# The quarters' normalisations read the broadcast root from its PSUM bank instead of a copy in SBUF

## The chip, the cores and the metric

The kernel runs on one core of one Trainium2 chip. The metric is device time in microseconds (us). Five things work side by side on a core: TensorE (PE, matrix products, with its weight loads as a row of their own, PEld), VectorE (DVE), ScalarE (ACT), GpSimd (POOL) and the DMA queues, which SyncE (SP) issues. SBUF is the working memory; PSUM is the memory that matrix products are written to, in banks of 512 columns of float32.

## The reference

One inference step of a streaming encoder with two layers, in float32, on 1024 frames of a new stream and 64 frames of a running one, with 1024 channels. Layer 0 is a state space mixer followed by a SwiGLU feed forward net, layer 1 is attention over a band of chunks followed by another one. Around every sub-layer stand two normalisations (this is the part that the change touches):

```python
def rmsnorm(x, w):
    xf = x.astype(jnp.float32)
    y = xf * lax.rsqrt(jnp.mean(xf * xf, axis=-1, keepdims=True) + EPS)
    return (y * w.astype(jnp.float32)).astype(x.dtype)

def swiglu(u, w_in, w_out):
    g, up = jnp.split(u @ w_in, 2, axis=-1)
    return (jax.nn.silu(g) * up) @ w_out

# per layer: m is the mixer or the attention of rmsnorm(x, nw[0])
x = x + rmsnorm(m, nw[1])
x = x + rmsnorm(swiglu(rmsnorm(x, nw[2]), ffn_w_in, ffn_w_out), nw[3])
```

## The kernel before

Activations are kept transposed: channels on the 128 partitions, in eight tiles of 128 channels, and frames along the columns. All 1088 frames (1024 and 64) are columns of one product, cut into three slices of 384, 384 and 320 columns or, in the feed forward part, into four quarters `QS` of 256, 256, 288 and 288 columns. Every product of float32 numbers is made of three (`passes`, L487): weights and activations are each split into a high part and a rest, by a cast on ACT and a subtraction on DVE (the weights' at L366 and L367, the activations' at L1214 and L1215, L1708 and L1709, L1802 and L1803).

A normalisation of a quarter goes through these steps. ACT squares each of the eight channel tiles (L517, L521) and POOL, in some places DVE, adds the squares up (`add_sq`, L522). PE sums over the partitions by products with a column of ones into a small PSUM tile `nst` (L529). Ten short DVE operations make the reciprocal root of it (`rstd`, L536 to L547). DVE spreads the root on a diagonal (`diag`, L558), and PE multiplies the diagonal with a constant matrix, so that each partition holds the root of every column: `nbp`, a PSUM bank (`bcast`, L566). ACT copies it to SBUF (L574), into a tile `rb` of which there is one only (`bufs=1`). Then DVE multiplies each of the eight channel tiles by the norm's weight (a column, one number for each partition) and by `rb` in one operation. `rb_steps` (L577) puts these steps together.

This is done in three places:

- `chain` (L1251), at the start of each feed forward part, for each of four quarters twice: the post norm of the mixer with x added (L1273 multiplies, L1274 adds, on DVE for odd tiles and on POOL for even ones), then the pre norm of the feed forward net (L1285). The second half of x is fetched by a DMA (L1270) once the first half has been added.
- `EndU` (L1780), at the end of layer 0, for each quarter: the post norm (L1845) with x added (L1846), then the squares of the sum, its split for layer 1 (L1802, L1803), and the root for layer 1's first norm, which goes into SBUF tiles `rba` that live on (the form of `bcast` with a list, L572). The quarters come in the order 0, 2, 1, 3.
- `end7` (L1749), at the end of layer 1, for quarters 0, 2 and 3 (L1760 multiplies, L1761 adds). Quarter 1 ends the kernel in another way (L1659 to L1680).

PE's order of instructions is the order in which the program is written out. `Stream` interleaves side tasks with PE's main work by estimated times: a task yields (cost, delay, condition). The constants `CHW`, `ER_W`, `EP_W`, `EQ_W`, `ER7` are such delays, so that PE does a broadcast only when its root is likely to be there. The order on the other engines is made by a scheduler when the program is built; `tc.high_priority(k)` moves work forward in it by k. `CHP` is 300 or 1500 for the chains, `ENP` is 0, 1500, 0, 1500 for the quarters 0 to 3 at the end of layer 0, `OPP` 0 or 1200 for the sums and splits that make the operands of the feed forward products (`op_build`), and `W.pri` 0 or 3000 for the weights' splits. The roots themselves have 3000 (`HIP`).

PSUM has eight banks. Two are `mm` (`pmm`), two are `ax` (`pax`: `nst`, `nbp` and small things), and in the feed forward part four belong to `px`. There `mm` is used by the products of `run_pair` (two of their four banks, L1484) and by layer 1's first units (L2229), but not by the projections, by `plain_pairs` or by the second products in `wino`, which use `px`.

Of the kernel before, what the change touches and what calls it, by code (L numbers as in the profile page):

```python
# [17 lines left out]
D = 1024  # L18
# [34 lines left out]
EP_W, ER_W, EQ_W = (3.0, 3.0, 3.0), (5.5, 7.0, 5.5, 4.5), (18.0, 2.5, 14.0, 22.0)  # L53
EP7, ER7 = (3.0, 0.0, 3.0, 2.5), (5.0, 4.0, 5.0, 4.5)
# [356 lines left out]
def hybrid_kernel(  # L411
# [65 lines left out]
    def ax(name):  # L477
        return pax.tile([P, 512], F32, tag="ax", name=name)
# [45 lines left out]
    def rstd(ssum, inv, r, nb, more=None, pad=False):  # L524

        sp, ts = ax("nst"), [ssum] if more is None else [ssum, more]
        for i in range(nb):
            for j, t in enumerate(ts):
                PE.matmul(  # L529
                    sp[:, i:i + 1], t[:, i * P:(i + 1) * P], ones[:, 0:1], start=(j == 0), stop=(j == len(ts) - 1)  # L530
                )
        with tc.high_priority(2 * HIP if pad else HIP):
            v = nsb.tile([P, 12], F32, tag="nv", bufs=2, name="nv")
            a, h, y = v[:, 0:nb], v[:, 4:4 + nb], v[:, 8:8 + nb]
            steps = [
                lambda: V.tensor_scalar(a, sp[:, :nb], inv, EPS, op0=ALU.mult, op1=ALU.add),  # L536
                lambda: V.tensor_scalar(
                    y.bitcast(I32), a.bitcast(I32), -0.5, float(0x5F3759DF), op0=ALU.mult, op1=ALU.add
                ),
                lambda: V.tensor_tensor(h, y, y, op=ALU.mult),  # L540
                lambda: V.tensor_tensor(h, h, a, op=ALU.mult),
                lambda: V.scalar_tensor_tensor(h, h, -10.0 / 3.0, h, op0=ALU.add, op1=ALU.mult),
                lambda: V.scalar_tensor_tensor(y, h, 5.0, y, op0=ALU.add, op1=ALU.mult),
                lambda: V.tensor_tensor(h, y, y, op=ALU.mult),
                lambda: V.scalar_tensor_tensor(a, h, 9.0 / 64.0, a, op0=ALU.mult, op1=ALU.mult),
                lambda: V.scalar_tensor_tensor(h, a, -10.0 / 3.0, a, op0=ALU.add, op1=ALU.mult),
                lambda: V.scalar_tensor_tensor(r, h, 5.0, y, op0=ALU.add, op1=ALU.mult),  # L547
            ]
            for k, f in enumerate(steps):
                i = f()  # L550
                if pad and k < 9:
                    with tc.issue_after(i.ins):
                        for c in (3, 7):
                            V.memset(v[:, c:c + 1], 0.0)
# [7 lines left out]

    def bcast(dg, a, n, rb=None):

        bp = ax("nbp")
        PE.matmul(bp[:, :n], frac, dg.rearrange("p a b -> p (a b)")[:, a:a + n], start=True, stop=True)  # L566
        DG.put()
        if rb is None:
            rb = nsb.tile([P, 384], F32, tag="rb", bufs=1, name="rb")
        elif isinstance(rb, list):  # L570
            for d, c0, c1 in rb:
                A.copy(d, bp[:, c0:c1])  # L572
            return None
        A.copy(rb[:, :n], bp[:, :n])  # L574
        return rb[:, :n]

    def rb_steps(ssum, n, out, wait=None, rb=None, more=None):  # L577

        nb = (n + P - 1) // P
        nr = nsb.tile([P, 4], F32, tag="nr", bufs=2, name="nr")  # L580
        rstd(ssum, 1.0 / D, nr[:, :nb], nb, more, rb is None or more is not None or isinstance(rb, list))
        yield 0.2, 0, DG.free
        with tc.high_priority(HIP):
            dg = diag(nr[:, :nb], nb)
        yield 0.1, wait or RB_WAIT
        with tc.high_priority(HIP):
            out.append(bcast(dg, 0, n, rb))
        yield 0.5, 0
# [117 lines left out]
    with ExitStack() as es:  # L706
# [406 lines left out]
        for s in range(NSL):  # L1113
            us, n = u[s], SL[s][1]
# [27 lines left out]
        for grp in order:  # L1142
# [6 lines left out]
            for i, s in seq:  # L1149
                kd_, jj_ = grp[i]  # L1150
                q = 3 * jj_ + s
# [99 lines left out]
    def chain(layer, q, y, ss, cw, xsrc, xout, cpre, done):  # L1251

        o, n = QS[q]

        rings = (RX, R) if q < 2 else (R,)

        def some():
            return any(r.free() for r in rings)

        w_post, w_rb, w_pre = CHW[layer][q // 2]  # L1260
        yield 0, w_post, some
        t, r = take(*rings)
        xr = v4(t, n)
        nc.sync.dma_start(xr, xsrc[:, 0:4, o:o + n])
        out = []
        yield from rb_steps(ss, n, out, w_rb)
        s2 = ssum_start(n)
        for m in range(KD):
            if m == 4:
                nc.sync.dma_start(xr, xsrc[:, 4:8, o:o + n])  # L1270
            ym = y[m // 4][:, m % 4, :]
            with tc.high_priority(CHP[layer][q // 2]):
                V.scalar_tensor_tensor(ym, ym, col(cw + m), out[0], op0=ALU.mult, op1=ALU.mult)  # L1273
                (V if m % 2 else G).tensor_tensor(ym, ym, xr[:, m % 4, :], op=ALU.add)  # L1274
                add_sq(s2, ym, n, m == 0)
            if m % 4 == 3:
                nc.sync.dma_start(xout[:, m - 3:m + 1, o:o + n], y[m // 4])
        r.put()
        yield 0, w_pre
        out = []  # L1280
        yield from rb_steps(s2, n, out, w_rb)
        for m in range(KD):
            ym = y[m // 4][:, m % 4, :]
            with tc.high_priority(CHP[layer][q // 2]):
                V.scalar_tensor_tensor(ym, ym, col(cpre + m), out[0], op0=ALU.mult, op1=ALU.mult)  # L1285
        done.append(q)
# [400 lines left out]
    def back(layer, start, cpost, xsrc, xmid, cpre, cpost2, xout, rb_out, done2):  # L1687
# [3 lines left out]
        with ExitStack() as es:  # L1691
# [57 lines left out]
            def end7(q, y, ss, more):  # L1749

                o, n = QS[q]
                yield 0, EP7[q], lambda: R.free(2)
                xs = [v4(R.get(), n) for _ in range(2)]
                for i in range(2):
                    nc.sync.dma_start(xs[i], xmid[:, 4 * i:4 * i + 4, o:o + n])
                out = []
                yield from rb_steps(ss, n, out, ER7[q])
                for m in range(KD):
                    ym, xm = y[m // 4][:, m % 4, :], xs[m // 4][:, m % 4, :]
                    V.scalar_tensor_tensor(ym, ym, col(cpost2 + m), out[0], op0=ALU.mult, op1=ALU.mult)  # L1760
                    V.tensor_tensor(ym, ym, xm, op=ALU.add)  # L1761
                    if m % 2:
                        nc.sync.dma_start(xout[:, m - 1:m + 1, o:o + n], y[m // 4][:, m % 4 - 1:m % 4 + 1, :])
                    yield 0, 0.3
                R.put(2)
                done7.add(q)
# [13 lines left out]
            class EndU:  # L1780
# [29 lines left out]
                def __call__(self, q, y, ss, more):  # L1810

                    o, n = QS[q]
                    last = q == 3
# [13 lines left out]
                        yield 0, EP_W[q], lambda: "in" in done7  # L1827
                        xs = [get(m) for m in range(4)]
                    out = []
                    yield from rb_steps(ss, n, out, ER_W[q], more=more)  # L1830
                    tot = [ssum_start(n) for _ in range(1 + last)]

                    def tail(m):
# [574 lines left out]
```

## Time and profile before

| what | us |
|---|---|
| median of 3 runs (lowest and highest) | 3044.62 (3039.18 to 3047.13) |
| the profiled execution, its time | 3046.02 |
| its span, first to last instruction | 3044.0 |
| PE busy (share of the span) | 2929.2 (96%) |
| DVE busy | 2318.2 (76%) |
| ACT busy | 1476.1 (48%) |
| POOL busy | 612.4 (20%) |
| mean granted clock of TensorE, as a share of full speed | 0.983 |

The profile gives the busy time of each engine, groups of instructions by line of the kernel, and for each idle time of an engine what ended it. In a row of the timeline the first number is the start in us after the first instruction, the second the length in us, then engine, line, operation, output and inputs, form and count; in square brackets the idle time before it and what ended that. A row of waits reads: who waited, for whom, total us, times, longest us. A row of one line's instructions gives the least, median and largest duration in ns.

### The profile page before, as it was taken

Reading aid. Unit: us, or ns where it says so; the run is one execution under the profiler, and the core shown is the slowest. Engines: PE = TensorE matmul, PEld = TensorE weight load, DVE = VectorE, ACT = ScalarE, POOL = GpSimd, SP = SyncE. Lnnn points to the kernel's source line nnn. Section 1 sums busy time; section 2 is a strip of 40 time slices with the busy share of each in tenths; the row PEclk is TensorE's granted clock in tenths of the full one; section 3 lists DMA queues with packets and bytes.
Section 4 is the critical chain, followed back from the end, with each engine's and each line's share of the span. In section 5 each row is a group of like instructions: output and inputs, shape, how many; then the busy total and the mean of one; then the engine's idle time right before and its main releaser. Section 6 shows DMA issues by size and latency. Waiting matters only on the chain. (4 is left out here: it accounts for less than half of the span.)

```text
span 3044.0 us, 60295 instructions
## 1 busy us (share of the span) xinstructions
PE 2929.2 (96%) x22295; PEld 2863.3 (94%) x22295; DVE 2318.2 (76%) x5669; ACT 1476.1 (48%) x2870; POOL 612.4 (20%) x774
## 2 busy tenths in 40 slices
PE   9899999999999999999997999999898999999998
PEld 8899999999999999999987989999798999999998
DVE  7988888885889677686687777777668867768567
ACT  5665656554444333345454555555543433335452
POOL 1334343431342122100130000000154111210011
PEclk9999999999999999999998999999998999999999
DMA  3333333335533555558774222122343456556665
GB/s 119 111 95 103 96 100 97 98 113 167 161 126 121 170 182 168 169 174 249 223 214 146 70 71 76 63 73 76 129 137 122 133 160 194 164 164 205 188 192 185
DMA packets 296536, 426.24 MB, mean 140 GB/s; under 512 B 31184, under 2 KB 250896, under 8 KB 296240
## 3 DMA queue, kind: packets, MB, share of 16 engines
q1 hardware_dynamic: 296176, 422.32, 44.1%
q8 instruction: 175, 2.87, 0.4%
q14 instruction: 121, 0.99, 0.1%
q0 software_dynamic: 64, 0.07, 0.0%
HBM read 309.81 MB, written 108.00 MB: 137 GB/s over the span
## 5 line engine op out<-in xcount | busy, mean ns | idle before, releaser
L495 PE MATMUL mm<-r,hl 128*128 128x384 f32 (+2 forms) x1632 | 550.1, 337 | 19.2 <-ACT r L2210 7.7
L496 PE MATMUL mm<-r,hl 128*128 128x384 f32 (+2 forms) x1632 | 530.9, 325 | 1.2 <-DVE r L2211 0.7
L497 PE MATMUL mm<-r,hl 128*128 128x384 f32 (+2 forms) x1632 | 530.9, 325 | 0.6 <-DVE hl L367 0.6
L1489 PE MATMUL px<-r,hl 128*128 128x288 f32 (+1 forms) x1192 | 350.8, 294 | 0.1
L367 DVE TENSOR_TENSOR hl<-raw,hl 128x1024 fp32r<-128x1024 f32 (+2 forms) x230 | 257.7, 1122 | 106.9 <-ACT hl L366 102.9
L495 PEld LDWEIGHTS mm<-r,hl 128*128 128x128 f32 x1632 | 312.3, 191 | 22.8 <-ACT r L2210 7.9
L496 PEld LDWEIGHTS mm<-r,hl 128*128 128x128 f32 x1632 | 312.2, 191 | 2.5 <-DVE r L1803 1.2
L1488 PE MATMUL px<-r,hl 128*128 128x288 f32 x1056 | 312.3, 296 | 1.6 <-ACT p L1499 1.6
L497 PEld LDWEIGHTS mm<-r,hl 128*128 128x128 f32 x1632 | 311.2, 191 | 1.0 <-DVE hl L367 1.0
L1490 PE MATMUL px<-r,hl 128*128 128x288 f32 x1056 | 311.6, 295 | 0.0
L366 ACT CAST hl<-raw 128x1024 fp32r<-128x1024 f32 (+2 forms) x230 | 216.9, 943 | 158.9 <-PE po L1588 52.9
L1488 PE MATMUL px<-rx,hl 128*128 128x256 f32 x816 | 230.3, 282 | 12.4 <-ACT p L1499 12.4
L522 POOL TENSOR_TENSOR ssum<-ssum,sq 128x288 f32<-128x288 f32 (+1 forms) x139 | 150.6, 1086 | 418.8 <-ACT sq L521 413.6
L1490 PE MATMUL px<-rx,hl 128*128 128x256 f32 x816 | 228.8, 280 | 0.1
L1489 PEld LDWEIGHTS px<-r,hl 128*128 128x128 f32 x1192 | 224.8, 189 | 0.5 <-DVE r L1215 0.3
L1488 PEld LDWEIGHTS px<-r,hl 128*128 128x128 f32 x1056 | 199.4, 189 | 2.6 <-ACT p L1499 2.1
L1490 PEld LDWEIGHTS px<-r,hl 128*128 128x128 f32 x1056 | 199.1, 189 | 0.0
L1588 PE MATMUL po<-rx,hl 128*128 128x256 f32 (+1 forms) x650 | 188.2, 290 | 3.3 <-DVE hl L367 3.3
L1489 PE MATMUL px<-rx,hl 128*128 128x256 f32 x680 | 190.8, 281 | 0.0
L1586 PE MATMUL po<-rx,hl 128*128 128x256 f32 (+1 forms) x650 | 189.0, 291 | 1.9 <-ACT p L1609 1.9
L1587 PE MATMUL po<-rx,hl 128*128 128x256 f32 (+1 forms) x650 | 187.6, 289 | 0.0
L1499 ACT COPY u<-px 128x288 f32<-128x288 f32 (+1 forms) x156 | 60.2, 386 | 222.6 <-PE px L1490 220.9
(422 smaller groups left out, 8615.8 us busy)
## 6 DMA issues: line engine op xcount, KB each, us to landing
raw<-in_w_f_dram SPq DMA_DIRECT2D x108, 512.0 KB, 3.8
sg<-hop SPq DMA_DIRECT2D x154, 144.0 KB, 3.2
sg<-hop SPq DMA_DIRECT2D x166, 128.0 KB, 3.0
raw<-in_w_in_dram SPq DMA_DIRECT2D x40, 512.0 KB, 3.4
raw<-in_w_so_dram SPq DMA_DIRECT2D x32, 512.0 KB, 3.8
sx<-in_w_f_dram SPq DMA_DIRECT2D x72, 192.0 KB, 2.9
wt<-sx SPq DMA_DIRECT2D x72, 192.0 KB, 2.8
dm<-acd SPq DMA_DIRECT2D x64, 192.0 KB, 3.7
```

Source lines behind the costliest of these rows:

```text
L366: self.last = self.nc.scalar.copy(h, v).ins
L367: (eng or self.eng or self.nc.vector).tensor_tensor(lo, v, h, op=ALU.subtract)
L495: PE.matmul(ps[:, :n], h_, xh, start=(first and i == 0), stop=False)
L496: PE.matmul(ps[:, :n], h_, xl, start=False, stop=False)
L497: PE.matmul(ps[:, :n], l_, xh, start=False, stop=(last and i == nk - 1))
L522: (eng or G).tensor_tensor(ssum[:, :n], ssum[:, :n], q[:, :n], op=ALU.add)
L1488: PE.matmul(ps, wh, ah[:, k, :], start=(k == 0 and not on), stop=False, skip_group_check=on)
L1489: PE.matmul(ps, wh, al[:, k, :], start=False, stop=False, skip_group_check=on)
L1490: PE.matmul(ps, wl, ah[:, k, :], start=False, stop=(k == 3), skip_group_check=on)
L1586: PE.matmul(ps[b][:, :n], wh, xh, start=(k == 0), stop=False)
L1587: PE.matmul(ps[b][:, :n], wh, xl, start=False, stop=False)
L1588: PE.matmul(ps[b][:, :n], wl, xh, start=False, stop=(k == KH - 1))
```

## The change

`bcast` and `rb_steps` take a function that gives a PSUM tile: `mm` or `ax`. If they are given one, the broadcast product is written into a tile of that pool, there is no copy by ACT, and the PSUM tile itself is returned, so that the eight multiplications read it there. `chain` gives `mm` for both of its norms; `EndU` gives `mm` for the quarters 0, 1 and 2 and `ax` for the last (quarter 3), and `end7` gives `ax`. The bank is held until the last of the eight multiplications has read it. The other uses of `bcast` (the norm at the start, the groups' norm of the mixer in `build_y`, the lists at the end of layer 0) are as before. The last argument of `rstd` (it decides on small writes between the short operations and on their priority) has the same value as before at every call.

```diff
     def bcast(dg, a, n, rb=None):
 
-        bp = ax("nbp")
+        bp = rb("rb") if callable(rb) else ax("nbp")
         PE.matmul(bp[:, :n], frac, dg.rearrange("p a b -> p (a b)")[:, a:a + n], start=True, stop=True)
         DG.put()
+        if callable(rb):
+            return bp[:, :n]
         if rb is None:
             rb = nsb.tile([P, 384], F32, tag="rb", bufs=1, name="rb")
         elif isinstance(rb, list):
...
-        rstd(ssum, 1.0 / D, nr[:, :nb], nb, more, rb is None or more is not None or isinstance(rb, list))
+        rstd(ssum, 1.0 / D, nr[:, :nb], nb, more, callable(rb) or isinstance(rb, list))
...
     def chain(layer, q, y, ss, cw, xsrc, xout, cpre, done):
...
-        yield from rb_steps(ss, n, out, w_rb)
+        yield from rb_steps(ss, n, out, w_rb, mm)
...
         yield 0, w_pre
         out = []
-        yield from rb_steps(s2, n, out, w_rb)
+        yield from rb_steps(s2, n, out, w_rb, mm)
...
             def end7(q, y, ss, more):
...
-                yield from rb_steps(ss, n, out, ER7[q])
+                yield from rb_steps(ss, n, out, ER7[q], ax)
...
             class EndU:
...
-                    yield from rb_steps(ss, n, out, ER_W[q], more=more)
+                    yield from rb_steps(ss, n, out, ER_W[q], ax if last else mm, more)
```

## The prediction

> **What bounds the kernel now.** I read the page first, then busy time by stage, then TensorE's (PE's) waits inside the stages that contain the changed normalisations.
>
> ```profile
> span 3044.0 us, 60295 instructions
> ...
> PE 2929.2 (96%) x22295; PEld 2863.3 (94%) x22295; DVE 2318.2 (76%) x5669; ACT 1476.1 (48%) x2870; POOL 612.4 (20%) x774
> ```
>
> ```profile
> 790.00:930.00 140.00, 138.37 (x1076) 136.74 (x1075) 118.26 (x327) 60.95 (x116) 61.98 (x62) 1.00 0.45 144
> 1550.00:1700.00 150.00, 128.63 (x789) 124.07 (x788) 125.34 (x442) 70.02 (x148) 29.45 (x37) 0.89 0.51 158
> 2230.00:2370.00 140.00, 122.46 (x913) 120.75 (x913) 118.77 (x358) 56.73 (x110) 64.81 (x64) 0.91 0.38 126
> 2970.00:3044.00 74.00, 66.36 (x520) 64.68 (x518) 51.46 (x183) 19.20 (x37) 12.25 (x13) 0.99 0.59 189
> ```
>
> Over the span PE is the bound (96% busy). The four rows of the second fence (stretch and its length, then busy time of PE, its weight loads, DVE, ACT and POOL, the granted clock, DMA) are the stages with changed work: the chains of layer 0 (790 to 930 us), the end of layer 0 (1550 to 1700), the chains of layer 1 (2230 to 2370) and the tail. In the first PE is idle for 1.6 us: what the normalisations cost there is hidden. In the second and third PE is idle for 21.4 and 17.5 us at a granted clock of 0.89 and 0.91. A change to DVE and ACT can move the end only in those two.
>
> What PE waited for in the second stage (first two rows) and the third (last three):
>
> ```profile
> PE nst L529 <- POOL ssum L522: 7.4, 3, 5.0
> PE mm L495 <- ACT r L1802: 6.5, 2, 4.5
> ...
> PE mmx L497 <- DVE hl L367: 9.6, 1, 9.6
> PE nbp L566 <- DVE dg L558: 3.0, 1, 3.0
> PE nst L529 <- POOL ssum L522: 2.9, 1, 2.9
> ```
>
> All of these end on DVE, or on POOL and ACT work fed by DVE, and a wait costs more than itself. After the 3.0 us one, which ends at 2266.9:
>
> ```profile
> 2268.00:2270.00 2.00, 2.00 (x10) 2.00 (x10) 1.11 (x1) 1.53 (x3) 1.61 (x3) 0.50 0.32 127
> ...
> 2274.00:2276.00 2.00, 2.00 (x15) 2.00 (x15) 1.98 (x9) 0.85 (x2) 0.67 (x2) 0.92 0.00 0
> ```
>
> PE is busy and granted half its clock for some 7 us, so that 3 us of waiting cost about 3 + 7 x 0.5 = 6.5.
>
> **The change part by part.** 23 normalisations are touched: 16 in the chains (2 layers x 4 quarters x 2), 4 at the end of layer 0, 3 in the tail. Each loses one ACT copy, and its eight DVE multiplications take the root from PSUM: 23 copies go, 184 multiplications change an operand. The matmuls and their number stay.
>
> *The copies.* 23 x about 0.39 us (row below) is 9.0 us of ACT, which was busy for 48% and is no bound: hidden under PE, I take nothing for the work. As a link between matmul and first multiplication a copy costs 0.4 us where DVE was already waiting for it.
>
> ```profile
> L574 ACT COPY rb<-nbp x42: 354/394/479, 30.1 to 3021.6; 128x288 f32<-128x288 f32 x20, 128x256 f32<-128x256 f32 x19, 128x384 f32<-128x384 f32 x2, 128x320 f32<-128x320 f32 x1
> 1646.17 0.52 DVE L1845 SCALAR_TENSOR_TENSOR p<-p,pcs,rb 128x288 f32<-128x288 f32 x1 [5.70 <-ACT rb L574]
> ```
>
> Most of that 5.70 is PE, which comes to the broadcast late; only the last 0.4 is the copy. I count this one hop, in the end of layer 0: 0.4. The other 22 stand behind DVE work or PE that sets the time.
>
> *The multiplications.* This is the large term. The same instruction has two prices now:
>
> ```profile
> L1273 DVE SCALAR_TENSOR_TENSOR rx<-rx,pcs,rb x32: 472/954/1032, 794.5 to 2254.4; 128x256 f32<-128x256 f32 x32
> 826.27 3.25 DVE L1285 SCALAR_TENSOR_TENSOR rx<-rx,pcs,rb 128x256 f32<-128x256 f32 x8
> 926.77 3.52 DVE L1285 SCALAR_TENSOR_TENSOR r<-r,pcs,rb 128x288 f32<-128x288 f32 x8
> L839 DVE SCALAR_TENSOR_TENSOR cvt<-craw,pcs,cvt x216: 535/608/1225, 37.8 to 639.6; 128x384 f32<-128x384 f32 x72, 128x323 f32<-128x323 f32 x36
> L976 DVE SCALAR_TENSOR_TENSOR y<-xsT,pcs,yp x48: 531/602/616, 103.7 to 659.6; 128x384 f32<-128x384 f32 x32, 128x320 f32<-128x320 f32 x16
> ```
>
> A multiplication of 256 columns takes 472 ns or about 950. Eight in a row while POOL is idle take 3.25 us (3.52 at 288); the doubled ones lie beside POOL adds. The pair that decides is L839 and L976, the same operation in the same stage: with both tensors in SBUF it reaches 1225 ns, with the second tensor (yp) in PSUM it never passed 616. So I take it that a root in PSUM ends the doubling. Undisturbed the PSUM form is no dearer: least and median 531 and 602 against 535 and 608 at nearly the same widths. I take 0 for the operand itself, with bounds from -6 to +6 ns, 1.1 us over 184.
>
> [...]
>
> How much doubling each stage holds: the busy time of L1273 alone (first two rows), of L1285 (third) and of L1845 (last three).
>
> ```profile
> 2236.00:2264.00 28.00, 11.16 (x16) 1.00 0.52 171
> 2297.00:2330.00 33.00, 11.49 (x16) 0.77 0.41 129
> 2264.00:2297.00 33.00, 8.24 (x16) 0.86 0.29 101
> 1550.00:1583.00 33.00, 5.62 (x8) 0.90 0.72 217
> 1583.00:1613.00 30.00, 5.05 (x8) 1.00 0.62 189
> 1613.00:1640.00 27.00, 4.63 (x8) 0.61 0.62 191
> ```
>
> Undisturbed, 16 take 6.5 us (7.0 at 288 columns). Chains of layer 1: 11.16 - 6.5 = 4.7, 8.24 - 6.5 = 1.7 and 11.49 - 7.0 = 4.5, in sum 10.9 us of DVE ahead of the weight split that ends the 9.6 us wait. That split stands in order behind them, with POOL's adds beside:
>
> ```profile
> 2317.68 8.33 POOL L522 TENSOR_TENSOR ssum<-ssum,sq 128x288 f32<-128x288 f32 x7
> ```
>
> ```profile
> 2317.95 3.94 DVE L1273 SCALAR_TENSOR_TENSOR r<-r,pcs,rb 128x288 f32<-128x288 f32 x4
> ...
> 2323.87 3.21 DVE L367 TENSOR_TENSOR hl<-raw,hl 128x1024 fp32r<-128x1024 f32 x2
> 2325.41 0.58 PE L497 MATMUL mmx<-rx,hl 128*128 128x256 f32 x1 [9.63 <-DVE hl L367]
> 2259.04 1.31 DVE L1274 TENSOR_TENSOR rx<-rx 128x256 f32<-128x256 f32 x2 [1.98 <-DMA rx<-x2d]
> ```
>
> What counts is how much earlier that split ends. The upper bound is the whole 10.9. The lower is 1.7: DVE's waits for DMAs (1.98 in the last row), for casts and for PE's own broadcasts take up the rest. DVE is busy for 85% of the stage and PE's earlier wait (3.0, with its half clock 6.5) goes with the same work, so I lean to the upper end: 8 us. Next late after it is the POOL add that ended the 2.9 us wait; it is shut out by op_build's two-operand SBUF work, which the change leaves.
>
> End of layer 0: 5.62 - 3.25, 5.05 - 3.52 and 4.63 - 3.25 are 2.4 + 1.5 + 1.4 = 5.3 us of DVE, plus the hop of 0.4. Part of it goes into DVE's waits for weights there, of which the trace gives no single price. I take about half of 5.7 less that part, 2.5; the order of two quarters (below) sets its bounds, 0 and 6.5.
>
> Chains of layer 0: PE idles 1.6 us in all; I take 0.5, bounds 0 and 1.6. Tail: DVE was busy 51 of 74 us and PE 66; I take 0, with 1 us either way.
>
> *Banks and order.* Two waits are new. A root now holds a bank of mm (or ax) until its eighth multiplication, so the broadcast after next, and any unit in mm, waits for DVE, and all of PE stands behind it. The nearest meeting:
>
> ```profile
> 1627.87 0.47 DVE L1845 SCALAR_TENSOR_TENSOR r<-r,pcs,rb 128x256 f32<-128x256 f32 x1
> 1631.58 0.45 PE L496 MATMUL mm<-r,hl 128*128 128x384 f32 x1 [0.56 <-DVE r L1803]
> 2361.71 0.50 DVE L1285 SCALAR_TENSOR_TENSOR r<-r,pcs,rb 128x288 f32<-128x288 f32 x1
> 2367.90 0.39 PE L1488 MATMUL px<-rx,hl 128*128 128x256 f32 x1 [2.10 <-ACT p L1499]
> ```
>
> Quarter 1's root is read until 1628.3; the unit that needs its bank comes after one that itself needs all of quarter 1's splits (still waiting at 1631.6). In layer 1 the last read ends at 2362.2, and the second mm bank of the products is wanted after 2367.9. Price 0, with 3 to 6 us of margin; without it, what DVE is late by. In the tail the roots lie in ax, and the sums between them take its other bank. Quarters that finish earlier also issue the second half of their x (the DMA of the 1.98 us wait) and their stores earlier on SP; at a DMA share of 0.38 in that stage I price that at 0.
>
> A wait is also gone: rb was one tile, so a norm's copy waited for the norm before to be read out.
>
> ```profile
> 1611.26 0.51 DVE L1845 SCALAR_TENSOR_TENSOR c<-c,pcs,rb 128x288 f32<-128x288 f32 x1
> 1611.80 0.37 ACT L574 COPY rb<-nbp 128x256 f32<-128x256 f32 x1 [0.21 <-DVE c L1845]
> 1613.79 1.94 DVE L1845 SCALAR_TENSOR_TENSOR r<-r,pcs,rb 128x256 f32<-128x256 f32 x2
> 1616.44 1.44 PE L529 MATMUL nst<-ones,ssum 128*128 128x1 f32 x6 [4.99 <-POOL ssum L522]
> 1624.01 0.69 PE L495 MATMUL mm<-r,hl 128*128 128x384 f32 x1 [4.48 <-ACT r L1802]
> ```
>
> Quarter 1's copy started when quarter 2's last multiplication ended. Now quarter 1, whose work has priority 1500 against quarter 2's 0, may run first, 5 us earlier. PE needs quarter 2 first (the sum at 1616.4), then quarter 1 (the units at 1624). So this order is worth between a gain of the 6.5 us waits on L1802 and a loss, priced as a rival.
>
> *Sum:* 8 + 2.5 + 0.5 + 0 = 11.0 us. The profiled execution took 3046.0 (span 3044.0 and 2.0 around it), so it becomes 3035.0; the median of the runs is 1.4 lower, which gives 3033.6, in round numbers **3034**. The forecast's own range, from 1.7 + 0 to 10.9 + 6.5 + 1.6 + 1 with the clock coming back in part (3 more), is 3021.5 to 3043.
>
> **Rivals.** *Quarter 1 overtakes quarter 2 on DVE.* In the rows above quarter 1's multiplications, with the adds and splits between them, run from 1613.79 to 1628.3: at most 14.5 us that would stand in front of quarter 2's last multiplications. The sum at 1616.4 would then come up to 14.5 us later, and the half clock after a wait costs some 1.7 more (half of the 7 us seen above, at half the loss): 16.2. If the later waits on L1802 (6.5) go in exchange, 9.7 is left. Against the 8 of layer 1 it decides from 8 us of lateness on: 3044.6 - 8 + 9.7 = 3046 to 3053, and to 3061 where the same two things, a wait that is gone and a priority of 1500, also put layer 1's multiplications further ahead of its weight split. For it: the priorities; against it: quarter 2 may be through when quarter 1's root is there, since its multiplications lose their doubling too.
>
> *The gain stays off PE's path.* DVE gets shorter, but PE goes on to be released by the POOL add (2.9 us), by DMAs and by casts: 1.7 + 0.4 + 0.5, about 3042. For it: the DVE waits for DMAs and casts above; against it: the 9.6 us wait with full DVE in front of it.
>
> *A PSUM operand is dearer than it looks.* The widest that the rows allow is the slowest L976 against the fastest L839, 616 - 535 = 81 ns. In the two stages that bind there are 32 + 32 multiplications, 5.2 us, and the gain falls to 5.8: 3039. For it: only that one row bears the form; against it: equal medians. [...]
>
> *The doubling stays*, because it hangs on something other than the second SBUF operand. Only the hops remain: 3044. Against it: L976 beside L839.
>
> **How the numbers follow.** Forecast 0.54, overtaking 0.18, off the path 0.18, dearer operand 0.04, doubling stays 0.06. About 0.3%, 9 us, is what a measurement of this kernel can tell from no change: faster means below 3035.5, slower above 3053.8. Of the forecast I lay five sixths below 3035.5, because the clock recovers with each wait that goes and the sum has that at 0: 0.45, and 0.03 from the other cases, so 0.48 faster. Slower is a good half of overtaking and a little for other orders of DVE, 0.12; the rest, 0.40, is the same. The range, 3021 to 3050, holds the forecast, the three neutral rivals and half of overtaking.
>
> **What would show it.** Multiplications at L1273, L1285, L1760 and L1845 with no duration above about 560 ns; 19 copies instead of 42 at L574; PE's wait on the weight split near 2315 under 5 us, and no half clock near 2270. Wrong: doubled multiplications with a PSUM root; PE waiting for a DVE multiplication before a broadcast or a unit in mm; in the end of layer 0 quarter 1's multiplications ahead of quarter 2's last, with a wait above 8 us before the sum.

## The result, and the profile after

The kernel after takes 3018.11 us (median of 6 runs, 3013.49 to 3020.84) against 3043.21 us before (6 runs, 3039.18 to 3047.13): a ratio of 0.9918, 95% interval 0.9905 to 0.9930, or 25 us (21 to 29). The forecast was 3034, the range 3021 to 3050; the result lies 3 us below the range. The sign came out, and the mechanism of the largest term; the size of that term and two smaller terms did not. The profiled execution took 3020.84 us, 25.2 less than the one before.

The page's line of the engines (busy time, share of the span, instructions):

```profile
PE 2919.1 (97%) x22295; PEld 2854.0 (95%) x22295; DVE 2289.9 (76%) x5669; ACT 1468.6 (49%) x2847; POOL 598.1 (20%) x774
```

PE has the same 22295 matmuls and is busy for 10.1 us less (2929.2 before). The mean granted clock rises from 0.983 to 0.987; an estimate from that alone, 2929.2 x 0.983 / 0.987, gives 2917. So some 10 of the 25 us are clock, and the other 15 are waiting that is gone.

The changed multiplications of layer 1's chains and all copies that are left, grouped by line and shape (least, median and greatest duration in ns, first and last start); numbers of lines are higher by 2 in this kernel:

```profile
L1275 DVE SCALAR_TENSOR_TENSOR rx<-rx,pcs,rb x16: 468/469/480, 2233.4 to 2244.7; 128x256 f32<-128x256 f32 x16
L1287 DVE SCALAR_TENSOR_TENSOR rx<-rx,pcs,rb x16: 469/470/476, 2262.9 to 2274.0; 128x256 f32<-128x256 f32 x16
L1275 DVE SCALAR_TENSOR_TENSOR r<-r,pcs,rb x16: 501/503/507, 2295.1 to 2309.6; 128x288 f32<-128x288 f32 x16
L1287 DVE SCALAR_TENSOR_TENSOR r<-r,pcs,rb x16: 499/508/515, 2328.6 to 2342.3; 128x288 f32<-128x288 f32 x16
...
L576 ACT COPY rb<-nbp x19: 354/400/481, 28.7 to 831.3; 128x256 f32<-128x256 f32 x8, 128x288 f32<-128x288 f32 x8, 128x384 f32<-128x384 f32 x2, 128x320 f32<-128x320 f32 x1
```

None is doubled, although POOL's adds run beside them as before. PE's waits in and behind the chains of layer 1, before (first four rows) and after:

```profile
PE mmx L497 <- DVE hl L367: 9.6, 1, 9.6
PE px L1488 <- ACT p L1499: 6.2, 2, 4.1
PE nbp L566 <- DVE dg L558: 3.0, 1, 3.0
PE nst L529 <- POOL ssum L522: 2.9, 1, 2.9
```

```profile
PE mmx L496 <- DVE rx L1217: 6.3, 1, 6.3
PE px L1490 <- ACT p L1501: 3.1, 1, 3.1
...
PE rb L566 <- DVE dg L558: 0.5, 1, 0.5
PE nst L529 <- POOL ssum L522: 0.4, 1, 0.4
```

The 9.6 us wait on the weight split is gone, those on the diagonal and POOL's sum are down to 0.5 and 0.4, and a wait of 6.3 us on the low half of an operand split (L1217) is new. Since PE's matmuls stand in the same order in both kernels, a stage can be bounded by the starts of the same matmuls. This gives the stage in four parts, before and after (stretch, length, then busy time of PE, its weight loads, DVE, ACT and POOL, the granted clock, DMA):

```profile
2230.02:2276.03 46.01, 43.06 (x299) 42.43 (x298) 38.01 (x149) 21.64 (x49) 28.94 (x35) 0.93 0.38 127
2276.03:2300.13 24.10, 21.25 (x153) 20.99 (x152) 23.31 (x83) 11.84 (x18) 8.75 (x5) 0.89 0.29 100
2300.13:2330.03 29.90, 20.27 (x147) 19.85 (x146) 27.16 (x33) 10.65 (x23) 20.33 (x20) 0.80 0.44 139
2330.03:2430.11 100.08, 93.74 (x732) 92.38 (x731) 79.62 (x165) 39.83 (x65) 19.87 (x15) 0.97 0.38 124
```

```profile
2225.59:2265.79 40.20, 39.81 (x299) 39.30 (x299) 29.99 (x136) 19.41 (x43) 28.28 (x32) 1.00 0.44 146
2265.79:2293.37 27.58, 20.82 (x153) 20.33 (x152) 27.36 (x99) 15.38 (x23) 5.47 (x8) 0.89 0.27 86
2293.37:2311.31 17.94, 17.94 (x146) 17.73 (x146) 17.12 (x28) 8.03 (x18) 13.07 (x15) 0.99 0.62 204
2311.31:2408.53 97.22, 93.04 (x731) 91.57 (x730) 80.33 (x168) 38.65 (x64) 24.73 (x20) 0.98 0.41 132
```

The lengths change by -5.8, +3.5, -12.0 and -2.9: **17.1 us**, where the sum had 8. PE's busy time falls by 3.3, 0.4, 2.3 and 0.7, in sum 6.7; what PE is not busy falls from 21.8 to 11.3, by 10.5. The rest of the 25.2 lies in layer 0's chains (2.5), the tail (2.9) and, unevenly, in the end of layer 0 and between.

How much of this is clock can be read directly. The trace records the granted clock, and in both kernels each record of it is full or half (1.00 or 0.50). The stretches at half clock in the stage, before (first four rows) and after:

```profile
2267.51:2274.33 6.82, 6.82 (x30) 6.82 (x30) 5.28 (x29) 4.74 (x10) 6.14 (x8) 0.50 0.39 144
2294.82:2301.63 6.81, 6.78 (x31) 6.78 (x32) 5.31 (x58) 2.26 (x3) 0.09 (x1) 0.50 0.07 22
2318.71:2328.94 10.23, 3.53 (x16) 3.54 (x17) 10.23 (x10) 3.04 (x7) 9.87 (x9) 0.50 0.60 178
2407.46:2414.28 6.82, 5.80 (x25) 5.81 (x26) 6.04 (x12) 2.44 (x5) 0.19 (x1) 0.50 0.64 204
```

```profile
2287.07:2293.89 6.82, 4.32 (x20) 4.32 (x21) 6.82 (x9) 4.67 (x6) 0.00 (x0) 0.50 0.19 68
2389.47:2392.87 3.40, 3.40 (x17) 3.40 (x16) 3.33 (x7) 1.55 (x4) 0.00 (x0) 0.50 0.75 241
```

PE is busy at half clock for 22.9 us before and 7.7 after; half of the difference is 7.6 us, near the 6.7 by which its busy time falls. In three profiles that leave this stage as it was (before, only_end0, l0_tail, below) it is 15.6 to 23.0 us, in five with the change here (after, after_again, after_q2, no_end0, only_l1) 4.6 to 7.8.

The order on DVE changed too. It follows from the priorities and the build's own estimate of when each instruction can run, so taking the copies out moves other instructions. Before, the weight split that PE waited for 9.6 us stood behind all the multiplications of the half (at 2323.87); after, the same split, by its place among those of L367, is the first of these rows and stands ahead of them:

```profile
2291.71 1.22 DVE L367 TENSOR_TENSOR hl<-raw,hl 128x1024 fp32r<-128x1024 f32 x1
...
2293.98 1.22 DVE L367 TENSOR_TENSOR hl<-raw,hl 128x1024 fp32r<-128x1024 f32 x1
2295.11 0.93 DVE L1275 SCALAR_TENSOR_TENSOR r<-r,pcs,rb 128x288 f32<-128x288 f32 x2
```

So three things changed at once: where the operand lies, a copy less, and another order. The experiments take them apart.

### The profile page after: what moved, and what is told of

It is laid out like the page before. It is cut to its first block, busy times and chain, and to the rows that moved or that the text cites. A ratio compares the mean times of both kernels' runs of the same rounds, so it can differ in the third digit from the quotient of the medians.

```text
span 3019.1 us, 60270 instructions
## 1 busy us (share of the span) xinstructions
PE 2919.1 (97%) x22295; PEld 2854.0 (95%) x22295; DVE 2289.9 (76%) x5669; ACT 1468.6 (49%) x2847; POOL 598.1 (20%) x774
## 5 line engine op out<-in xcount | busy, mean ns | idle before, releaser
L367 DVE TENSOR_TENSOR hl<-raw,hl 128x1024 fp32r<-128x1024 f32 (+2 forms) x230 | 255.8, 1114 | 118.7 <-ACT hl L366 117.4
L522 POOL TENSOR_TENSOR ssum<-ssum,sq 128x288 f32<-128x288 f32 (+1 forms) x139 | 142.5, 1028 | 410.3 <-ACT sq L521 404.4
L1589 PE MATMUL po<-rx,hl 128*128 128x256 f32 (+1 forms) x650 | 187.1, 288 | 0.0
```

What stands on the lines that cost most here:

```text
L367: (eng or self.eng or self.nc.vector).tensor_tensor(lo, v, h, op=ALU.subtract)
L522: (eng or G).tensor_tensor(ssum[:, :n], ssum[:, :n], q[:, :n], op=ALU.add)
L1589: PE.matmul(ps[b][:, :n], wh, xl, start=False, stop=False)
```

## The experiments

For each kernel I give the stage of layer 1's chains between the same two matmuls (2230.02 and 2430.11 in the kernel before), from the view by stretches, in us:

| kernel | length | PE busy | PE not busy |
|---|---|---|---|
| before | 200.1 | 178.3 | 21.8 |
| after | 182.9 | 171.6 | 11.3 |
| only_l1 | 183.3 | 171.8 | 11.5 |
| copyps_l1 | 183.7 | 171.8 | 11.9 |
| nopool_l1 | 182.6 | 172.0 | 10.6 |
| sbufop_l1 | 193.2 | 174.5 | 18.7 |
| sb2_l1 | 200.5 | 176.6 | 23.9 |
| wpri_before | 197.6 | 177.7 | 19.9 |
| wpri_after | 187.1 | 173.6 | 13.4 |
| opp_q2 | 185.0 | 173.5 | 11.4 |

Two kernels that leave this stage as it was (only_end0 and l0_tail, below) have 199.5 and 198.7, so the stage repeats within about 2 us.

### Operand, copy or order: four kernels

*only_l1*: the chains of layer 1 alone (against the kernel after; the second norm likewise, `end7` and `EndU` as before).

```diff
-        yield from rb_steps(ss, n, out, w_rb, mm)
+        yield from rb_steps(ss, n, out, w_rb, mm if layer else None)
...
```

> The change made in the eight normalisations of layer 1's chains alone; the end of layer 0, layer 0's chains and the tail keep the copy. Theory A (the multiplications lose their doubling, and DVE with them) and theory B (the gain comes from the new order on DVE and ACT that follows from the missing copy) both expect some 17 us of the change's 25: 3026 us, 3022 to 3031. If the parts lean on one another (a stage that ends earlier only pays because a later one does too), the gain is under 12: above 3031. PE's wait on the weight split near 2315 gone, as with the whole change.

Measured 3027.67 us, ratio 0.9947 (0.9927 to 0.9967), and 16.8 us in the stage: the 17 are this part's own, and don't lean on the others.

*copyps_l1*: the copy stays, but into another PSUM bank. Against the kernel before; layer 1's chains give `mm`, and `bp` lies in `ax`.

```diff
-        if rb is None:
+        if callable(rb):
+            rb = rb("rb")
+        elif rb is None:
...
         A.copy(rb[:, :n], bp[:, :n])
```

> As only_l1, but the root is still made in ax and still copied by ACT, into another PSUM bank (mm) instead of SBUF; the multiplications read that PSUM copy. Copy and hop stay, and the order of the instructions on DVE, ACT and PE stays near the one before; only the operand's memory differs. Theory A: multiplications of layer 1's chains at 465 to 515 ns, 12 to 17 us faster, 3027 to 3032. Theory B (order and hop): no more than 4 us faster, 3040 or above.

Measured 3031.97 us, ratio 0.9960 (0.9947 to 0.9974). Its multiplications of 288 columns behind the first broadcast:

```profile
L1275 DVE SCALAR_TENSOR_TENSOR r<-r,pcs,rb x16: 502/504/515, 2304.9 to 2316.1; 128x288 f32<-128x288 f32 x16
```

With ACT's copies kept, 16.4 of the 17.1 us are there: beside only_l1 the copy and its hop are worth 0.4 us in this stage. (The median is 4.3 us above that of only_l1; their intervals overlap, and in the two profiles that difference lies outside this stage.) The order on DVE did not stay as expected: the weight split stands ahead of the multiplications here too, at 2299.93. So this run takes the copy out of the account, and not the order.

*sbufop_l1*: no copy, an order near that of only_l1, but the second tensor lies in SBUF. The normalisations of layer 1's chains leave out every token's root but the first, and the weights.

```diff
-                V.scalar_tensor_tensor(ym, ym, col(cw + m), out[0], op0=ALU.mult, op1=ALU.mult)
+                V.scalar_tensor_tensor(ym, ym, out[0][:, 0:1] if layer else col(cw + m), const[0][:, :n] if layer else out[0], op0=ALU.mult, op1=ALU.mult)
...
```

Here `const[0]` is an SBUF tile of ones.

> As only_l1 (no copy, the root stays in its bank of mm, order near that of only_l1), but the root enters the multiplications only as one PSUM column in the place of the per-partition weight, and the second tensor operand is a tile of ones in SBUF: the eight normalisations of layer 1 leave out the root of every token but the first, and the weights. Theory A: multiplications beside POOL's adds are doubled again (800 to 1050 ns), and most of the gain is lost: 3038 or above. Theory B: as only_l1, 3022 to 3031, doubled or not.

Measured 3035.98 us, ratio 0.9979 (0.9966 to 0.9991). The same group:

```profile
L1280 DVE SCALAR_TENSOR_TENSOR r<-r,rb x16: 509/1052/1067, 2303.9 to 2323.0; 128x288 f32<-128x288 f32 x16
```

The doubling is back, and 10.3 of the 17.1 us are lost. A single PSUM column as the scalar doesn't prevent it (1052 ns in the median); a whole tensor in PSUM did (504 in copyps_l1). The 6.9 us that remain fall between the theories: the split stands ahead here too (2291.18).

*nopool_l1*: kernel before, with POOL's residual adds of the even rows and the adds of the squares left out of layer 1's chains.

```diff
-                (V if m % 2 else G).tensor_tensor(ym, ym, xr[:, m % 4, :], op=ALU.add)
-                add_sq(s2, ym, n, m == 0)
+                if m % 2 or not layer:
+                    (V if m % 2 else G).tensor_tensor(ym, ym, xr[:, m % 4, :], op=ALU.add)
+                if m == 0 or not layer:
+                    add_sq(s2, ym, n, m == 0)
```

> Kernel before with POOL's work in layer 1's chains left out: the residual adds of the even rows and the adds of the squares (the normalisations there miss them). The copy, the root in SBUF and the order on DVE stay. Theory A (it is POOL's adds that double a two-SBUF multiplication): the multiplications of layer 1's chains take 465 to 515 ns with the root in SBUF, the wait near 2315 shrinks below 3 us, and the kernel is 12 us faster or more, 3032 or below. Theory B, or doubling by something else: durations up to 950 ns stay, and the gain is below 6 us.

Measured 3025.15 us, ratio 0.9939 (0.9921 to 0.9957). The same group:

```profile
L1273 DVE SCALAR_TENSOR_TENSOR r<-r,pcs,rb x16: 510/514/518, 2293.5 to 2303.6; 128x288 f32<-128x288 f32 x16
```

With the root in SBUF, copied, and the weight split behind these multiplications as before (at 2305.51), the doubling goes when POOL's adds go, and the stage is 17.5 us shorter, as with the change. In all four groups 6 of the 64 multiplications are still doubled (21 before), and each lies beside a POOL operation on two tensors that was left in. This shows that POOL's adds are the other party. The 17.5 us themselves are not a pure measure of the doubling, since this run also takes away POOL's own lateness at the sums. In these three kernels the multiplications of this group take 504 ns in the median with one tensor in PSUM (copyps_l1), 1052 with both in SBUF beside POOL's adds (sbufop_l1), and 514 with both in SBUF and those adds left out (nopool_l1).

### One tile, or the order alone

*sb2_l1*: two SBUF tiles for the root instead of one, in layer 1's chains.

> Kernel before with two SBUF tiles for the root in layer 1's chains instead of one, until the pool that holds them is closed (the first two quarters and the start of the others): a norm's copy no longer waits for the norm before to be read out. Copy, root in SBUF and doubling stay, the order of the instructions nearly too. If the single tile was part of the 17 us: 3 us faster or more, 3040 or below. If not: within 2 us of before, 3041 to 3045, and multiplications up to 1050 ns.

Measured 3044.57 us, ratio 0.9998 (0.9988 to 1.0008), and 200.5 us in the stage. The single tile was no part of it.

*wpri_before* and *wpri_after*: one line in the kernel before and in the kernel after, which puts the weight splits ahead by priority.

```diff
+                W.pri = 2000 if layer else 0
                 ops[0].yring, ops[1].yring = RX, R
```

> Kernel before with one more line: in layer 1 the weight splits get priority 2000 while the chains run (before: 0, behind the chains' 1500 and the operand sums' 1200). Copy, root in SBUF and doubling stay; only the order changes, so that no weight split stands behind the multiplications. If a good part of the gain is order: the 9.6 us wait on the split goes, 5 to 9 us faster, 3035 to 3039. If the doubled work only shows up at the next wait (casts, the diagonal, the operands' splits): under 3 us, 3041 or above.

> Kernel after with the weight splits of layer 1 at priority 2000 while the chains run (as wpri_before is the kernel before with it). If the order carries a gain of its own, it adds to the change: 3 us faster than the kernel after or more, 3014 or below. If it carries one only where a split stands behind doubled work: within 2 us of the kernel after, 3015 to 3020, or slower where the splits push the roots back.

Measured 3040.56 us, ratio 0.9987 (0.9976 to 0.9997), and 3026.31 us, ratio 0.9944 (0.9927 to 0.9961). PE's waits in the stage of wpri_before:

```profile
PE px L1488 <- ACT p L1499: 6.3, 2, 4.8
PE mmx L496 <- DVE r L1215: 4.9, 1, 4.9
PE nbp L566 <- DVE dg L558: 4.5, 1, 4.5
PE mmx L496 <- DVE rx L1215: 2.9, 1, 2.9
```

The 9.6 us wait is gone by order alone, and the stage is 2.5 us shorter, not 10, hardly more than the 2 us within which it repeats: the same DVE work is late at the diagonal and at the operands' splits instead. On top of the change the line costs 4 us in the stage and 8 in the median. Order alone moves the lateness (21.8 us not busy become 19.9); work taken off DVE removes about half of it (11.3).

*opp_q2*: in the kernel after, the operand splits of layer 1's first half ahead of the roots (priority 7000 for 1200), and quarter 2 ahead in the end of layer 0 (below).

> The kernel after with two priorities changed: quarter 2 of the end of layer 0 at 2000 (as in after_q2), and the operand splits of layer 1's first half at 7000 instead of 1200, ahead of the roots. The new 6.3 us wait at 2283 to 2289 (PE on an operand split that stands behind two roots and a weight split) should fall below 3 us, with 1 to 3 us of clock behind it: 4 to 8 us faster than the kernel after, 3009 to 3014. If the split is late for its cast on ACT, which stands behind a cast that waits for a weight's DMA, the wait stays and only quarter 2's part shows: 3013 to 3018.

Measured 3023.05 us (6 runs) beside 3016.72 (5 runs) of the kernel after on the same chip:

```profile
PE rb L566 <- DVE dg L558: 4.8, 2, 4.4
...
PE mmx L496 <- DVE rx L1217: 1.8, 1, 1.8
```

The new wait falls from 6.3 to 1.8, and the diagonal of the roots, pushed back, takes 4.8. The miss is the same one: I priced the wait and not what is late next.

### The end of layer 0

*only_end0*: the four normalisations there alone. *after_q2*: the kernel after with one priority changed. *no_end0*: the whole change without this stage, timed beside *after_again*, the kernel after. The edit of after_q2:

```diff
-LDP, ENP, ATP = 1500, (0, 1500, 0, 1500), 1000
+LDP, ENP, ATP = 1500, (0, 1500, 2000, 1500), 1000
```

> The change made in the four normalisations of the end of layer 0 alone. If the stage's part is its own: 2 to 3 us faster, 3040 to 3041, with PE's wait on POOL's sum near 1604 to 1615 grown to about 11 us and the 6.5 us waits on the cast at the units nearly gone, as with the whole change (quarter 1's multiplications ahead of quarter 2's last). If that stage only gains with the others' change, 0 within 1 us.

> Kernel after with quarter 2 of the end of layer 0 at priority 2000 instead of 0, ahead of quarter 1 (1500). If the 10.9 us wait before the sum is quarter 1's overtaking, it shrinks below 6 us, the waits of the units on quarter 1's casts come back (about 6 us), and the time is within 3 us of the kernel after: 3015 to 3021. If quarter 2's lateness is POOL's adds and not the order, the 10.9 us stay.

> The whole change but for the end of layer 0, whose four normalisations keep the copy. If that stage's part is what its own matmuls show (0.4 us to 1635, for what quarter 1's overtaking gives back): within 1.5 us of the kernel after. If it is what the runs of the stage alone said (5.5 us, 3 to 9): 4 us or more slower than the kernel after.

> The kernel after, once more, on the chip of the three runs beside it, so that they can be set against it: 3018 us, 3014 to 3022.

Measured: only_end0 3037.67 us, ratio 0.9980 (0.9970 to 0.9990); after_q2 3015.53 us, ratio 0.9909 (0.9892 to 0.9925); no_end0 3018.80 us, ratio 0.9915 (0.9903 to 0.9928), against 3016.72, ratio 0.9907 (0.9893 to 0.9921), of after_again. PE's waits between 1550 and 1700, after (first two rows, and then the multiplications of quarters 1 and 2 ahead of the longer one) and in after_q2:

```profile
PE nst L529 <- POOL ssum L522: 12.4, 2, 10.9
...
PE mm L495 <- ACT r L1804: 1.3, 1, 1.3
...
1607.48 2.04 DVE L1847 SCALAR_TENSOR_TENSOR r<-r,pcs,rb 128x256 f32<-128x256 f32 x5
...
1609.81 0.93 DVE L1847 SCALAR_TENSOR_TENSOR c<-c,pcs,rb 128x288 f32<-128x288 f32 x2
```

```profile
PE mm L495 <- ACT r L1804: 6.7, 2, 5.3
...
PE nst L529 <- POOL ssum L522: 2.6, 2, 1.4
```

Quarter 1 (r) does overtake quarter 2 (c): its last five multiplications run ahead of quarter 2's last two, and the wait before the sum grows from 5.0 to 10.9 us, while the 6.5 us waits on quarter 1's casts fall to 1.3. With quarter 2 ahead both come back. after_q2 is 1.2 to 2.6 us below the two medians of the kernel after, inside their intervals: no measurable gain. What the stage as a whole is worth stays open between 0 and some 5 us: the stage alone gained 3 to 9 us, and leaving it out of the change cost 2.1 us by the medians. The profiles show no gain in its first half: between the matmuls at 1550.04 and 1630.59 (before) it takes 79.7 to 80.8 us in the nine without the change here and 79.8 to 81.3 in six with it. With quarter 2 ahead (after_q2, opp_q2) it takes 76.4 and 77.7, and the rest, to 1700.09, then takes 69.9 and 69.8 against 65.5 to 68.8 in those six: what the sum gains, the units' waits give back.

### Layer 0's chains and the tail

*l0_tail*: the change in these two alone.

> The change made in layer 0's chains and in the tail alone. With the whole change PE's stream came out 2.5 us ahead in layer 0's chains and 3.7 us in the tail. If both are the change's own: 5 to 7 us faster, 3036 to 3038, with the same steps at the same instructions. If they are spread between executions (the tail of the kernel with layer 1's chains alone came out 0.6 us behind): below 3 us in sum, 3040 or above.

Measured 3037.84 us, ratio 0.9982 (0.9972 to 0.9991), 5.5 us (3 to 9). The stage of layer 0's chains between the same matmuls in l0_tail, and in only_l1, which leaves it as it was:

```profile
785.94:959.22 173.28, 168.53 (x1321) 166.66 (x1320) 138.57 (x397) 74.62 (x132) 59.87 (x65) 1.00 0.42 140
```

```profile
785.68:960.40 174.72, 170.29 (x1322) 168.25 (x1321) 151.32 (x397) 76.98 (x140) 66.44 (x65) 0.99 0.43 138
```

In seven kernels with the change in layer 0's chains this stage is 1.8 to 2.9 us shorter than in the profile of before, in the seven others between 0.3 shorter and 1.5 longer: 2.8 us between the means. From the matmul at 2960 (before) on, the seven with the change in the tail are 2.6 to 4.4 us shorter, the seven others between 2.2 shorter and 1.7 longer: 2.9 us between the means. Both are the change's own.

### What a wait costs beside its length

*stall2* and *stall5*: the kernel after with six added waits, the first still inside the chains of layer 1, the others behind them, where PE is busy without a break at full clock.

```diff
+    def stall(k):
+        d = nsb.tile([P, 384], F32, tag="rb", bufs=1, name="rb")
+        z = ax("zz")
+        PE.matmul(z[:, :P], ones, ones, start=True, stop=True)
+        with tc.high_priority(HIP):
+            G.memset(d, 1.0)
+            A.copy(d[:, :P], z[:, :P])
+            for _ in range(k):
+                G.tensor_tensor(d, d, d, op=ALU.add)
+        z = ax("zz")
+        PE.matmul(z[:, :P], ones, d[:, :P], start=True, stop=True)
...
+                    if layer and 2 <= i < 8:
+                        stall(2)
                     run_pair(t_, W.get(), bs, ends, ops, hid, px, tmp, i == 0)
```

In stall5 the call is `stall(5)`.

> Kernel after with six added waits of TensorE in the 150 us of layer 1 behind 2430, where it is otherwise busy without a break at full clock: a small matmul, an ACT copy of its result, two POOL adds on that, and a matmul that waits for them; about 3 us each. If a wait costs only its length: 18 to 20 us slower than the kernel after, 3036 to 3038, and the same matmuls take the same busy time. If half clock follows each wait as in the stage of the chains (3.0 us of waiting that cost 6.5): 30 to 40 us slower, 3048 to 3058, with 2 to 4 us of added busy time behind each.

> As stall2 with five POOL adds, about 6 us for each wait. If a wait costs only its length: 36 us slower than the kernel after, 3054. If half clock follows and its cost does not depend on the wait's length: 48 to 58 us slower, 3066 to 3076; if it grows with the wait: above 3076.

Measured 3064.95 us, ratio 1.0082 (1.0061 to 1.0103), and 3080.33 us, ratio 1.0122 (1.0107 to 1.0138): 47 and 62 us above the kernel after. The waits came out longer than I had set them: five of 5.1 us in stall2 and of about 8 us in stall5, and the first longer still (10.7 and 13.1). The stretch in the kernel after; then in stall2 one wait's aftermath; then in stall5:

```profile
2408.00:2533.00 125.00, 125.00 (x1005) 125.00 (x1005) 88.81 (x156) 43.90 (x84) 24.94 (x18) 1.00 0.55 177
```

```profile
2444.50:2448.50 4.00, 4.00 (x20) 4.00 (x20) 0.00 (x0) 0.37 (x1) 0.42 (x1) 0.50 0.24 86
2448.50:2450.50 2.00, 2.00 (x14) 2.00 (x13) 0.00 (x0) 0.34 (x1) 0.00 (x0) 0.71 0.00 0
```

```profile
2421.00:2423.00 2.00, 2.00 (x11) 2.00 (x11) 0.00 (x0) 0.00 (x0) 0.42 (x1) 0.50 0.00 0
```

PE is busy behind the wait and runs at half clock (0.50 in both). Against the kernel after, the 168 matmuls behind each of the five waits take 1.1 to 2.5 us longer in stall2 and 1.2 to 2.6 in stall5 (mean of the ten 1.7), nearly all of it in the first 20 to 40. So a wait here costs its length and on average 1.7 us more, whether it lasts 5 or 8 us. An estimate from the shortest stretch of half clock in the traces of before and after, 3.41 us, is half of it, 1.7 us for each wait, and the mean of the ten agrees. The traces show more than one length, though: in stall2 the recorded half clock lasts 3.4 us at the wait that ends at 2416 and 6.8 at the one that ends at 2444, a part of it passes while PE still waits, and 2.9 and 5.6 us of it fall on busy time.

## Why the prediction was right, and where it was wrong

**Doubling: right.** The pair that decided it (yp in PSUM never doubled) was a fair one, since 16 of the 32 multiplications of L976 with 384 columns lie for more than half of their time beside POOL work, and it carried over: the greatest of the 184 changed multiplications takes 515 ns. Nor is the PSUM operand dearer: 469 ns at 256 columns against 472, 503 to 508 at 288 against 510 (the median of L1285 before). The rival of the dearer operand is out. The kernel that copies to SBUF is the slower one, because the second SBUF operand meets POOL's adds: layer 1's multiplications of L1273 with 256 columns take 956 ns in the median before, 469 after, and 478 in nopool_l1, which copies too but leaves those adds out. The other two signs came too: 19 copies, and no half clock ahead of the matmul that stood at 2276 before (0.93 became 1.00).

**Chains of layer 1, 8 us: the step that failed, by its size.** The working turned DVE time into PE's waiting, bounds 1.7 to 10.9, and the waiting did fall by 10.5, near the upper end where I had leaned. But the first part had read from the profile that 3.0 us of waiting cost about 6.5, and the sum then put the clock at 0, with up to 3 us in the forecast's range alone. It measured 6.7. The long waits of the stage before are 3.0, 2.9, 9.6 and 4.1 us, and half clock stands behind each. Behind the added waits it costs 1.1 to 2.6 us, behind the 3.0 and 2.9 us ones 3.4 each: the 6.8 us of half clock begin as these waits end and fall on busy PE whole, while behind the longer ones a part passes in the wait itself (3.5 of 10.2 us are left behind the 9.6). In l0_tail, with this stage as before, waits of 3.2 and 3.6 us are followed by 3.4 us of half clock each (the stage's clock is 0.95 there and 0.92 before). So how many such lengths a wait sets off differs between executions, and why is open.

Inside that term two steps were wrong, and they worked against each other. The order of DVE was taken as given: the split was moved ahead in the build, and the whole 9.6 us went instead of a part. And the POOL add was to be late next: before, it took 5.79 us beside op_build's operations on DVE; after, none of these adds takes more than 1.81, and that wait fell from 2.9 to 0.4. Late next, by 6.3, is op_build's split at L1217, behind two roots and a weight split. wpri_before has that split ahead and the doubling, and gains 2.5 us; sbufop_l1, the same without the copies, 6.9; nopool_l1, with the split behind and hardly any doubling, 17.5. So the order explains the place of the waits and the smaller part of the gain.

**End of layer 0, 2.5 us: not refuted, for other reasons.** The overtaking that I priced as a rival took place, at the place and with the exchange that it named (the 6.5 us waits on L1802). It is also one of the signs that I had named for being wrong, a wait above 8 us before the sum (10.9). Its price was too high: PE waits for the sum 5.9 us longer, not up to 14.5, and 5.2 come back. So the 2.5 us did not come the way I had worked them out, from shorter DVE work ahead of that sum, and what the stage gives is open. Its second half, the same overtaking in layer 1, did not happen. The chance of "slower" didn't follow from the rival either: its price, 3046 to 3053, lies below the 3053.8 that slower was to mean, and only its last clause, to 3061, reaches above.

**Chains of layer 0, 0.5 us: wrong.** I read the idle time of 790 to 930, and the stage's cost stands behind that edge, in the first products:

```profile
946.93 0.58 PE L1488 MATMUL px<-rx,hl 128*128 128x256 f32 x1 [3.18 <-ACT p L1499]
```

```profile
942.08 0.39 PE L1490 MATMUL px<-rx,hl 128*128 128x256 f32 x1 [0.76 <-ACT p L1501]
```

The stage gains 2.5 to 2.8 us, over the bound of 1.6, and little of that is waiting: in the stage between the same matmuls PE is not busy for 4.8 us before and 4.0 after, since waits of 1.7 and 1.1 come in. Its busy time falls by 1.7. Behind the 3.18 us wait the clock is half for 3.4 us, in all eight profiles that keep the copies here for 3.4 us or more; in the nine with the change no half clock shows in the stage. So this term, too, was mostly clock.

**Tail, 0 with 1 us either way: wrong.** PE was idle for 7.6 of the 74 us shown there, and I counted nothing for it. It is worth 2.9 us by the means. Which of its small waits gives it isn't settled.

**Banks, 0: right.** No wait of PE on a multiplication before a broadcast or a unit shows in either stage. In layer 1's chains the single rb tile cost nothing either (sb2_l1).

The parts: 17.1, 2.8 and 2.9 are 22.8 of the 25; the 2 that are left may be the end of layer 0 or the spread between executions. "The gain stays off PE's path" and "the doubling stays" are out. Had the sum carried the 6.7 us of clock and layer 0's 2.8 in place of 0.5, it would have come to about 3025, inside the range's lower half and still some 7 us above the result.

## What to carry to other kernels

When a wait of PE goes, count its length and the slower matmuls behind it (here 1.1 to 3.4 us for each), and put that into the sum, not only into the range. Here a DVE multiplication with two tensors in SBUF took about 950 ns instead of 472 beside POOL's adds, so leaving one operand in PSUM was worth far more than the copy that it saves. A wait removed by moving work came back nearly whole at the next instructions in line (19.9 us of 21.8), those removed by shorter work about half (11.3); look for what comes back past the edge of the stage.

## What the runs showed of the hardware that was not expected

The clock's answer to a wait is not the same in each execution. In the end of layer 0, kernels with the same waits differ; from the unit at 1630 on, before and l0_tail, which leaves this stage as it was:

```profile
1630.59:1700.09 69.50, 64.65 (x359) 62.88 (x359) 50.18 (x196) 29.88 (x70) 1.06 (x7) 0.90 0.33 103
```

```profile
1629.43:1694.31 64.88, 60.03 (x359) 58.28 (x359) 50.15 (x196) 29.87 (x70) 1.05 (x7) 0.97 0.35 111
```

The same matmuls, the same 4.85 us not busy, and 4.6 us of busy time between them at a clock of 0.90 and 0.97: PE is busy at half clock for 13.4 us in the first and 3.4 in the second. Of the other profiles some have the long form (nopool_l1, and with the change in this stage after) and some the short one (wpri_before, sbufop_l1, and with the change only_end0). In the traces of before and after each stretch at half clock is 3.41 us long or a whole multiple of it (one to four times, 30 stretches), but for the last of each, at the end of the program (4.01 and 3.64); so each length more or less is worth up to 1.7 us of PE's time, an estimate from half of 3.41. A stage's gain of a few us in a single profile can be this alone, which is why the worth of the end of layer 0 stays open.
